# Two-layer hybrid backbone: the second layer's gate of the conditioning summed on VectorE, the first layer's on TensorE with 256 columns a group

## The chip, the cores and the metric

One core of a Trainium2 chip runs the whole forward pass as one program. The metric is the device time of one execution in microseconds (us), the median of the executions shown. Engine names are those of the profile: PE is TensorE's matmul, PEld its weight load, DVE is VectorE, ACT is ScalarE, POOL is GpSimd, SP is SyncE, which in this kernel issues nearly all DMAs, in one order.

## The reference, cut to what matters

`x` holds 1024 latent tokens and `ctx` 256 context tokens, both 1024 wide. Each of the two layers takes a shift, a scale and a gate from a conditioning vector. Context tokens have a conditioning vector of their own, and the second layer's context output is not needed.

```python
cond_l = silu(c)[:, None, :]          # latent tokens
cond_c = silu(c_ctx)[None, None, :]   # context tokens
for layer in range(2):
    shift_l, scale_l, gate_l = split(cond_l @ w_ada[layer] + b_ada[layer], 3)
    shift_c, scale_c, gate_c = split(cond_c @ w_ada[layer] + b_ada[layer], 3)
    hl = rms_norm(x, norm_g[layer]) * (1 + scale_l) + shift_l
    hc = rms_norm(xc, norm_g[layer]) * (1 + scale_c) + shift_c
    yl, yc = even_layer(hl, hc, ...) if layer == 0 else odd_layer(hl, hc, ...)
    x = x + gate_l * yl
    if layer == 0:
        xc = xc + gate_c * yc
return rms_norm(x, final_g)
```

`w_ada[layer]` is 1024 x 3072. So of the second layer's gate only the latent row counts, of the first layer's both rows.

## The kernel before

`run` (line 188) goes through the stages in order: `layer0_in`, `layer0_out`, `layer1_in`, `layer1_attention`, `layer1_out`. All products of activations and weights are made from a high and a low part (`mm3`, line 98: three matmuls, lines 100 to 102), with 512 columns for latent tokens (operand `h`) and 256 for context tokens (`h0c`).

The conditioning is computed inside `layer0_in`. The two conditioning vectors stand as two of 32 stationary columns in `cs` (line 253), one 128-row block `k` of eight after another. The first layer's shift and scale come from `ada_chunk` (line 262, matmuls of 256 columns at line 269). What is left are sixteen steps, made by `ada_steps` (line 411): eight for the second layer's shift and scale (bank 0, weights `w_ada1`) and then eight for the gates (bank 1, weights `w_adag`, in which each row holds 1024 columns of the first layer's gate and 1024 of the second's). Each step takes a block `wa` of 128 x 2048 (1 MB, loaded by `ada_load`, line 257, into one of three buffers) and makes four matmuls of 32 x 512 columns, one for each group of 32 columns of the array (`ada_step`, line 280, matmul at line 282), added up over the eight steps in one PSUM bank. Behind the eighth step `ada_end` (line 285) adds the bias `bt` (line 288). For bank 0 it transposes the sum (line 295) into the layer's scale and shift; for bank 1 it stores rows 0 and 1 of each group to `gate_d` in DRAM with four DMAs (line 291), which both layers later read back with `gate_tile` (line 305).

The steps are spread over the projections of the first layer: loop `j` over five weight blocks (K and four of Q, line 463), in each a loop over the token groups of 512, 512 and 256 columns, 24 matmuls to a group, with a step behind chunks 3 and 7 where the table `ADA` says so. A finished group goes to `rotated` (line 375): ACT copies it from PSUM to `qk` (line 380, three buffers), DVE shuffles it (383), POOL and DVE multiply by cosine and sine (384, 385), DVE adds (386), and a DMA stores it to `q_d` (388). The weight blocks are loaded as `raw` (line 146 or 130), cast on ACT to the high part (line 88, `w_hi`) and split on POOL (line 96, `w_lo`). Behind the steps come the weight block and the products of the next part, `sg` (lines 499 to 504), with Gelu on ACT.

In this stage no order is written out by hand: a scheduler that plans with a timeline of its own sets the order of instructions on every engine, from what is ready and from the order of the program. Every engine and SP then work in that order, so that an instruction that waits holds up all behind it on its engine. From the first layer's attention on (line 624) the order is the program's own.

Of the kernel before, what the change touches and what calls it, by code (L numbers as in the profile page):

```python
# [7 lines left out]
F32 = mybir.dt.float32  # L8
# [3 lines left out]
ALU = mybir.AluOpType  # L12
# [4 lines left out]
P = 128  # L17
D = 1024
KC = D // P
# [5 lines left out]
GROUPS = [(0, 512), (512, 512), (1024, 256)]  # L25
# [5 lines left out]
XB = 8  # L31
# [22 lines left out]
class Kernel:  # L54
# [227 lines left out]
            self.nc.tensor.matmul(ps[32 * g:32 * g + 32, 0:512], lhsT=self.cs[:, k, :],  # L282
                                  rhs=wa[:, g * 512:(g + 1) * 512], start=k == 0, stop=k == KC - 1)

    def ada_end(self, bank, ps):
        nc = self.nc
        at = self.t(self.wap, [P, 512], F32, "at", bufs=1)
        nc.vector.tensor_tensor(at, ps[:, 0:512], self.bt[:, bank], op=ALU.add)
        if bank == 1:
            for g in range(4):  # L290
                nc.sync.dma_start(self.gate_d[g], at[32 * g:32 * g + 2, :])
            return
        tp = ps
        for j in range(4):
            nc.tensor.transpose(tp[:, j * P:(j + 1) * P], at[:, j * P:(j + 1) * P], self.ident)
        ad = self.t(self.wap, [P, 4, 4, 2], F32, "ad", bufs=1)
        nc.vector.tensor_copy(ad, tp.rearrange("p (j g q) -> p j g q", j=4, g=4)[:, :, :, 0:2])
        for r in range(2):
            v = lambda a: a.rearrange("p (g j) -> p g j", g=2)
            w = lambda s: ad[:, :, s:s + 2, r].rearrange("p j g -> p g j")  # L300
            nc.vector.scalar_tensor_tensor(v(self.aT[1][:, r]), w(2), 1.0, v(self.ng[:, 1]),
                                           op0=ALU.add, op1=ALU.mult)
            nc.vector.tensor_copy(v(self.sT[1][:, r]), w(0))
# [8 lines left out]
    def layer0_in(self):  # L312
        nc, i = self.nc, self.i
# [5 lines left out]
        wp = self.pool(es_h, "w0")  # L319
# [16 lines left out]
        xp = self.pool(es_p, "xp", bufs=4, side="right")  # L336
        load_ = self.load
# [60 lines left out]
        def weights(j):  # L398
            return self.wblock(wp, i["w0"][8 + j], eng=("A", "G"), load=load_)

        ada = [(b, k) for b in range(2) for k in range(KC)]
        fetched = []

        def fetch(n):
            while len(fetched) < n and len(fetched) < len(ada):
                b, k = ada[len(fetched)]
                fetched.append(self.ada_load(i["w_ada1" if b == 0 else "w_adag"][k]))
# [3 lines left out]
        def ada_steps(n):  # L411
            for _ in range(n):
                if self.ada_done == len(ada):
                    return
                b, k = ada[self.ada_done]
                if k == 0:
                    self.ada_ps = self.psum("b", 2)
                fetch(self.ada_done + 2)
                self.ada_step(k, self.ada_ps, fetched[self.ada_done])
                self.ada_done += 1  # L420
                if k == KC - 1:
                    self.ada_end(b, self.ada_ps)


        xs = [xload(*GROUPS[0])]
        wa = [self.ada_load(i["w_ada0"][0])]
# [6 lines left out]
        ps = [self.bank() for _ in parts]  # L433
# [17 lines left out]
        load_(ca, i["ca"])  # L451
        load_(sa, i["sa"])
        for g in range(4):
            load_(self.bt[32 * g:32 * g + 2], i["bada"][g])
        fetch(2)
        norm(xs[2])
        for c in range(KC):
            modulated(xs[2], GROUPS[2], c)
            if c in ADA[0]:
                ada_steps(1)  # L460
        for b, (j, g, lag) in zip(ps, parts):
            rotated(j, b, GROUPS[g])
        for j in range(5):
            w = ws[j]
            for g, group in enumerate(GROUPS):
                if j < 2 and g < 2:
                    continue
                b = self.bank()
                for c in range(KC):
                    chunk(b, w, c, group)  # L470
                    if c in ADA[1 if j < 2 else 2 + g]:
                        ada_steps(1)
                rotated(j, b, group)
            if 0 < j < 4:
                ws.append(weights(j + 1))
        ada_steps(16)
        es_p.close()
        es_a.close()
        self.vt = self.pool(self.es_at, "v0", side="right").tile([P, NT, P], F32, name="vt")
# [16 lines left out]
        for hf in range(2):  # L496
            nc.sync.dma_start(bsb[64 * hf:64 * hf + 64], i["bs"][hf].partition_broadcast(64))

        w = self.wblock(wp, i["w0"][0])
        for j in range(4):  # L500
            wn = self.wblock(wp, i["w0"][j + 1]) if j < 3 else None
            for g0, gn in GROUPS:
                ps = self.project(w, hx, g0, gn)
                nc.scalar.activation(sg[:, j, g0:g0 + gn], ps, AF.Gelu)
            w = wn
            for k in WV[j]:
                raw = self.raw(i["wv"][k], [P, 640])
                self.hi("A", vwh[:, k], raw)
                self.lo("V", vwl[:, k], raw, vwh[:, k])
# [14 lines left out]
        for t in range(NT):  # L524
            ps = self.wide()
# [32 lines left out]
        bank = lambda: self.psum("b", 2)  # L558
# [1020 lines left out]
```

## Time and profile before

| | |
|---|---|
| median of three executions | 1503.92 us (1503.28 to 1504.01) |
| the profiled execution's own time | 1504.3 us |
| its span, first to last instruction | 1502.5 us |
| mean granted TensorE clock | 0.994 |
| PE busy | 1439.6 us, 96% |
| DVE busy | 879.5 us, 59% |
| ACT busy | 735.9 us, 49% |
| POOL busy | 397.4 us, 26% |

The span leaves 1.8 us of the execution outside the first and last instruction. Busy times are averages over stages; the conditioning steps all lie between 66 and 144 us of the span. In the timeline rows a matmul in fp32 shows as two records, so that a step of four matmuls reads x8 (x6 where records are missing), and the time that a step holds TensorE is read from the start of one matmul to the start of the next, since matmuls overlap in the rows.

### The profile page before, as it was taken

To read this page: it belongs to the slowest core of one execution; us is meant where nothing else is said; L and a number is where in the kernel's file an instruction comes from. 1 tells how busy PE (TensorE), PEld (TensorE's weight loads), DVE (VectorE), ACT (ScalarE), POOL (GpSimd) and SP (SyncE) were. 2 spreads that over 40 slices of the span, in tenths; PEclk is the share of its full clock that TensorE was granted. 3 is DMA by queue.
4 is the path that set the end of the run, shared out by engine and by line. 5 is a ranking of instruction groups with operands and counts; after the bars stand their busy time and mean duration, and the time that the engine had idled before them with its cause. 6 is when DMAs were issued, how large, how long until landed. Compare 5 with 4: busy or idle time off the path is not lost.

```text
span 1502.5 us, 23133 instructions
## 1 busy us (share of the span) xinstructions
PE 1439.6 (96%) x8849; PEld 1132.6 (75%) x8849; DVE 879.5 (59%) x1690; ACT 735.9 (49%) x1563; POOL 397.4 (26%) x351
## 2 busy tenths in 40 slices
PE   5999999999999799999998999999999999999998
PEld 3766899777666478879887777777777777776786
DVE  5582124356667877543745766676667666766454
ACT  4422310145567635443435766666666666676321
POOL 4243233223556533232470110011001100124100
PEclk9999999999999999999999999999999999999999
DMA  8557401222214646321231000000000000212241
GB/s 329 230 219 272 136 29 29 85 81 85 72 39 155 188 123 191 130 76 57 71 127 39 24 24 15 25 24 24 15 25 24 24 15 22 71 46 81 96 144 71
DMA packets 83783, 132.64 MB, mean 88 GB/s; under 512 B 7552, under 2 KB 59976, under 8 KB 80600
## 3 DMA queue, kind: packets, MB, share of 16 engines
q1 hardware_dynamic: 83528, 130.91, 25.9%
q8 instruction: 69, 1.13, 0.3%
q14 instruction: 42, 0.34, 0.1%
q10 hardware_dynamic: 144, 0.26, 0.0%
HBM read 99.59 MB, written 31.56 MB: 87 GB/s over the span
## 4 chain that ended last, share of the span: by engine, by line
PE 75%; DVE 9%; ACT 5%; issue 4%; DMA 4%; POOL 2%; SPq 0%; POOLq 0%; DVEq 0%; ACTq 0%
PE acc L1270 9%; PE tm L1252 7%; PE s L100 7%; PE s L101 7%; PE s L102 7%; PE b L100 5%; PE b L101 4%; PE b L102 4%; PE s L1215 3%; PE s L1216 3%; PE s L1217 3%; PE tm L100 2%; PE acc L774 2%; DVE peak L1227 2%; ACT prob L1242 2%
## 5 line engine op out<-in xcount | busy, mean ns | idle before, releaser
L1259 ACT COPY pt<-tm 128x512 f32<-128x512 f32 x192 | 112.4, 585 | 165.7 <-PE tm L1252 165.7
L1252 PE MATMUL tm<-ident,prob 128*128 128x128 f32 x1280 | 178.3, 273 | 7.8 <-ACT pt L1259 2.1
L1252 PEld LDWEIGHTS tm<-ident,prob 128*128 128x128 f32 x1280 | 150.8, 140 | 42.0 <-PE tm L1252 9.5
L1242 ACT ACTIVATE prob<-s,peak 128x1024 f32<-128x1024 f32 x128 | 143.3, 1120 | 38.0 <-DVE peak L1231 29.6
L1227 DVE TENSOR_REDUCE peak<-s 128x1 f32<-128x1024 f32 x128 | 155.0, 1211 | 1.8 <-PE s L1217 1.7
L1270 PE MATMUL acc<-pt,v 128*64 128x256 f32 x1280 | 152.0, 384 | 0.0
L96 POOL TENSOR_TENSOR ql<-pe,qh 32x512 fp32r<-32x512 f32 x32 | 40.7, 1271 | 413.2 <-ACT qh L88 386.2
L1261 DVE COPY pt<-tm 128x512 f32<-128x512 f32 x128 | 87.8, 686 | 79.4 <-PE tm L1252 77.4
L96 POOL TENSOR_TENSOR w_lo<-raw,w_hi 128x512 fp32r<-128x512 f32 (+1 forms) x60 | 74.9, 1261 | 199.0 <-DVE w_hi L90 98.5
L1270 PEld LDWEIGHTS acc<-pt,v 128*64 128x64 f32 x1280 | 86.3, 136 | 49.7 <-issue 9.6
L1215 PE MATMUL s<-kh,qh 96*128 96x512 f32 x256 | 109.2, 426 | 2.5 <-DVE raw L186 1.5
L1216 PE MATMUL s<-kl,qh 96*128 96x512 f32 x256 | 100.9, 394 | 0.0
L1217 PE MATMUL s<-kh,ql 96*128 96x512 f32 x256 | 100.8, 394 | 0.0
L1168 DVE TENSOR_TENSOR ql<-tm,qh 64x256 fp32r<-64x256 f32 x62 | 26.1, 421 | 83.7 <-ACT qh L1166 83.3
L100 PE MATMUL b<-h,yh 128*128 128x512 f32 x160 | 63.8, 399 | 3.7 <-ACT yh L88 2.7
L100 PE MATMUL s<-h,w_hi 128*128 128x512 f32 x160 | 63.9, 412 | 2.2 <-ACT qk L380 2.2
L101 PE MATMUL s<-h,w_hi 128*128 128x512 f32 x160 | 63.7, 398 | 0.3 <-DVE rs_v L125 0.3
L101 PE MATMUL b<-h,yh 128*128 128x512 f32 x160 | 63.3, 395 | 0.0
L102 PE MATMUL s<-h,w_lo 128*128 128x512 f32 x160 | 63.0, 395 | 0.0
L102 PE MATMUL b<-h,yl 128*128 128x512 f32 x160 | 62.5, 391 | 0.0
L1242 ACT ACTIVATE prob<-sx,peak 128x256 f32<-128x256 f32 x128 | 61.0, 477 | 0.6
L1217 PEld LDWEIGHTS s<-kh,ql 96*128 96x128 f32 x256 | 48.0, 188 | 11.2
(469 smaller groups left out, 3733.7 us busy)
## 6 DMA issues: line engine op xcount, KB each, us to landing
wa<-in_w_ada_dram SPq DMA_DIRECT2D x16, 1024.0 KB, 9.1
x<-in_xs_dram SPq DMA_DIRECT2D x20, 512.0 KB, 5.6
raw<-in_w_dram SPq DMA_DIRECT2D x17, 512.0 KB, 3.6
wa<-in_w_adag_dram SPq DMA_DIRECT2D x8, 1024.0 KB, 5.9
raw<-in_w_out_dram SPq DMA_DIRECT2D x10, 512.0 KB, 3.9
yf<-y_d SPq DMA_DIRECT2D x10, 512.0 KB, 5.6
x_d<-x SPq DMA_DIRECT2D x8, 512.0 KB, 4.5
raw<-in_w1g_dram SPq DMA_DIRECT2D x8, 512.0 KB, 3.4
```

The lines of the kernel that those rows point to most:

```text
L96: e.tensor_tensor(lo, src, hi.bitcast(F32), op=ALU.subtract)
L100: mm(out, lhsT=ah, rhs=bh, start=start, stop=False)
L101: mm(out, lhsT=ah, rhs=bl, start=False, stop=False)
L102: mm(out, lhsT=al, rhs=bh, start=False, stop=stop)
L1215: mm(o, lhsT=qh[0:96, q], rhs=kh[0:96, k0:k1], start=True, stop=False)
L1216: mm(o, lhsT=qh[0:96, q], rhs=kl[0:96, k0:k1], start=False, stop=False)
L1217: mm(o, lhsT=ql[0:96, q], rhs=kh[0:96, k0:k1], start=False, stop=True)
L1227: nc.vector.reduce_max(m[:, 0, a:a + 1], banks[n, a], axis=AX.X)
L1242: nc.scalar.activation(probs[n][j][:, TL:T] if c else probs[n][j][:, 0:TL], src, AF.Exp, bias=peaks[n][:, 2, j:j + 1], scale=scale, accum_ ...
L1252: nc.tensor.transpose(tp[:, o * P:(o + 1) * P], probs[n][j][:, k * P:(k + 1) * P], self.ident)
L1259: nc.scalar.copy(dst, src)
L1270: mm(accs[m][64 * e:64 * e + 64, 0:QG], lhsT=self.v4[hp // 2][:, kt, vc:vc + 64], rhs=pts[2 * m + e][:, kt], start=kt == 0, stop=kt == NT - 1)
```

## The change

The eight gate steps compute the two halves of a `wa` block in two ways. The first layer's 1024 columns go to TensorE as before, as four matmuls of 256 columns a step (`ada_gate_step`). The second layer's 1024 columns go to DVE: each step multiplies the 128 x 1024 half by the block's conditioning column (128 x 1) and adds it to a running total `ada_total`, which takes a buffer of the tag `x`. After the eighth step, `ada_gates` sums the total over its 128 partitions with four matmuls of 256 columns whose stationary operand is the constant `ones`, into the other half of the same bank, adds the bias, and stores eight pieces of 256 columns to `gate_d` in place of four of 512. The bias `bt` is loaded in twelve pieces in place of four. `ada_gates` stands behind the weight block and the first 512-column group of the next part's first product (`front`), which are moved ahead of the closing of the pools.

```diff
-    def ada_end(self, bank, ps):
+    def ada_gate_step(self, k, ps, total, wa):
+
+        nc = self.nc
+        for g in range(4):
+            nc.tensor.matmul(ps[32 * g:32 * g + 32, 0:256], lhsT=self.cs[:, k, :], rhs=wa[:, g * 256:(g + 1) * 256],
+                             start=k == 0, stop=k == KC - 1)
+        if k == 0:
+            nc.vector.tensor_scalar_mul(total, wa[:, D:2 * D], self.cs[:, k, 0:1])
+        else:
+            nc.vector.scalar_tensor_tensor(total, wa[:, D:2 * D], self.cs[:, k, 0:1], total, op0=ALU.mult, op1=ALU.add)
+
+    def ada_gates(self, ps, total):
+        nc = self.nc
+        for g in range(4):
+            nc.tensor.matmul(ps[32 * g:32 * g + 32, 256:512], lhsT=self.ones, rhs=total[:, g * 256:(g + 1) * 256],
+                             start=True, stop=True)
+        at = self.t(self.wap, [P, 512], F32, "at", bufs=1)
+        nc.vector.tensor_tensor(at, ps[:, 0:512], self.bt[:, 1], op=ALU.add)
+        for g in range(4):
+            c = slice(g % 2 * 256, g % 2 * 256 + 256)
+            nc.sync.dma_start(self.gate_d[g // 2][:, c], at[32 * g:32 * g + 2, 0:256])
+            nc.sync.dma_start(self.gate_d[2 + g // 2][:, c], at[32 * g:32 * g + 2, 256:512])
+
+    def ada_end(self, ps):
         nc = self.nc
         at = self.t(self.wap, [P, 512], F32, "at", bufs=1)
-        nc.vector.tensor_tensor(at, ps[:, 0:512], self.bt[:, bank], op=ALU.add)
-        if bank == 1:
-            for g in range(4):
-                nc.sync.dma_start(self.gate_d[g], at[32 * g:32 * g + 2, :])
-            return
+        nc.vector.tensor_tensor(at, ps[:, 0:512], self.bt[:, 0], op=ALU.add)
...
-                self.ada_step(k, self.ada_ps, fetched[self.ada_done])
+                wa = fetched[self.ada_done]
                 self.ada_done += 1
+                if b == 1:
+                    if k == 0:
+                        self.ada_total = self.t(xp, [P, D], F32, "x", bufs=XB)
+                    self.ada_gate_step(k, self.ada_ps, self.ada_total, wa)
+                    continue
+                self.ada_step(k, self.ada_ps, wa)
                 if k == KC - 1:
-                    self.ada_end(b, self.ada_ps)
+                    self.ada_end(self.ada_ps)
...
         for g in range(4):
-            load_(self.bt[32 * g:32 * g + 2], i["bada"][g])
+            load_(self.bt[32 * g:32 * g + 2, 0], i["bada"][g, :, 0])
+            c = slice(g % 2 * 256, g % 2 * 256 + 256)
+            load_(self.bt[32 * g:32 * g + 2, 1, 0:256], i["bada"][g // 2, :, 1, c])
+            load_(self.bt[32 * g:32 * g + 2, 1, 256:512], i["bada"][2 + g // 2, :, 1, c])
...
         ada_steps(16)
+        w = self.wblock(wp, i["w0"][0])
+        front = [self.project(w, hx, *GROUPS[0])]
+        self.ada_gates(self.ada_ps, self.ada_total)
         es_p.close()
         es_a.close()
...
-        w = self.wblock(wp, i["w0"][0])
         for j in range(4):
             wn = self.wblock(wp, i["w0"][j + 1]) if j < 3 else None
             for g0, gn in GROUPS:
-                ps = self.project(w, hx, g0, gn)
+                ps = front.pop(0) if front else self.project(w, hx, g0, gn)
                 nc.scalar.activation(sg[:, j, g0:g0 + gn], ps, AF.Gelu)
```

The scheduler's order changes with it between 66 and 146 us; from there on it is the same but for a few casts on ACT. Two places follow. Line numbers grow by 19 inside `layer0_in` of the changed kernel (383 becomes 402, 385 becomes 404, 386 becomes 405, 288 becomes 311, 388 becomes 407), and numbers behind names only tell one buffer from the next.

DVE's order before, where the fourth and fifth rotated groups of Q (`qk_984` and `qk_1073`) are followed by the bias of bank 0 (`at`):

```order
L383 STREAM_SHUFFLE hf_986<-qk_984 128x512
L385 TENSOR_TENSOR hf_986<-hf_986,x_689 128x512
L386 TENSOR_TENSOR qk_984<-qk_984,hf_986 128x512
L383 STREAM_SHUFFLE hf_1075<-qk_1073 128x512
L385 TENSOR_TENSOR hf_1075<-hf_1075,x_689 128x512
L386 TENSOR_TENSOR qk_1073<-qk_1073,hf_1075 128x512
L288 TENSOR_TENSOR at_1100<-b_916,bt 128x512
L383 STREAM_SHUFFLE hf_1133<-qk_1131 128x512
```

Here nothing but a rotation's own operands stands between its shuffle and its sum. The same place in the changed kernel:

```order
L402 STREAM_SHUFFLE hf_994<-qk_992 128x512
L404 TENSOR_TENSOR hf_994<-hf_994,x_689 128x512
L405 TENSOR_TENSOR qk_992<-qk_992,hf_994 128x512
L402 STREAM_SHUFFLE hf_1083<-qk_1081 128x512
L292 TENSOR_SCALAR x_1135<-wa_1102,cs 128x1024
L404 TENSOR_TENSOR hf_1083<-hf_1083,x_689 128x512
L405 TENSOR_TENSOR qk_1081<-qk_1081,hf_1083 128x512
L311 TENSOR_TENSOR at_1108<-b_924,bt 128x512
L294 SCALAR_TENSOR_TENSOR x_1135<-wa_1133,cs,x_1135 128x1024
L402 STREAM_SHUFFLE hf_1143<-qk_1141 128x512
L294 SCALAR_TENSOR_TENSOR x_1135<-wa_1162,cs,x_1135 128x1024
```

The first gate block's multiplication (L292, which needs the loaded `wa_1102`) now stands inside the rotation of `qk_1081`, and the next two additions stand around the shuffle behind it.

SP's order of DMAs before, from the last two blocks of bank 0 (`wa_1049`, `wa_1067`) to the weight block of loop `j` = 4 (`raw_1173`); `wa_1094`, `wa_1125`, `wa_1152` are the first three gate blocks:

```order
L130 DMA wa_1049<-in_w_ada_dram 128x2048
L130 DMA wa_1067<-in_w_ada_dram 128x2048
L130 DMA wa_1094<-in_w_adag_dram 128x2048
L388 DMA q_d<-qk_890 128x256
L388 DMA q_d<-qk_822 128x512
L388 DMA q_d<-qk_939 128x512
L388 DMA q_d<-qk_1023 128x256
L388 DMA q_d<-qk_984 128x512
L130 DMA wa_1125<-in_w_adag_dram 128x2048
L388 DMA q_d<-qk_1073 128x512
L130 DMA wa_1152<-in_w_adag_dram 128x2048
L130 DMA raw_1173<-in_w_dram 128x1024
```

Here the first gate block's load goes out ahead of the five stores. The same place in the changed kernel, where `wa_1102`, `wa_1133`, `wa_1162` are the first three gate blocks and `raw_1184` is the weight block of `j` = 4:

```order
L130 DMA wa_1057<-in_w_ada_dram 128x2048
L130 DMA wa_1075<-in_w_ada_dram 128x2048
L407 DMA q_d<-qk_898 128x256
L407 DMA q_d<-qk_830 128x512
L407 DMA q_d<-qk_947 128x512
L407 DMA q_d<-qk_1031 128x256
L407 DMA q_d<-qk_992 128x512
L130 DMA wa_1102<-in_w_adag_dram 128x2048
L130 DMA wa_1133<-in_w_adag_dram 128x2048
L407 DMA q_d<-qk_1081 128x512
L130 DMA wa_1162<-in_w_adag_dram 128x2048
L130 DMA raw_1184<-in_w_dram 128x1024
```

The first gate block's load has moved behind five stores of rotated groups, and the third gate block and the weight block stand behind the store of `qk_1081` as before.

## Rows read from the trace of the kernel before

**Rows 1.** The page: busy time of the engines, and the chain that ended last.
```profile
PE 1439.6 (96%) x8849; PEld 1132.6 (75%) x8849; DVE 879.5 (59%) x1690; ACT 735.9 (49%) x1563; POOL 397.4 (26%) x351
...
PE 75%; DVE 9%; ACT 5%; issue 4%; DMA 4%; POOL 2%; SPq 0%; POOLq 0%; DVEq 0%; ACTq 0%
```

**Rows 2.** Busy by stretch: length, each engine busy (count), clock, DMA share, GB/s.
```profile
100.00:120.00 20.00, 20.00 (x117) 12.79 (x116) 11.37 (x22) 3.08 (x6) 9.50 (x6) 1.00 0.72 270
120.00:140.00 20.00, 20.00 (x112) 13.42 (x111) 5.32 (x8) 4.98 (x9) 9.11 (x7) 1.00 0.80 315
```

**Rows 3.** Timeline of PE around a gate step: start, length, what [idle before <- releaser].
```profile
128.71 0.39 PE L102 MATMUL s<-h,w_lo 128*128 128x512 f32 x1
129.03 1.06 PE L282 MATMUL b<-wa,cs 128*32 128x512 f32 x8
...
130.36 0.39 PE L101 MATMUL s<-h,w_hi 128*128 128x512 f32 x1
```

**Rows 4.** Timeline of PE around four matmuls of 256 columns in `ada_chunk`.
```profile
51.94 0.40 PE L102 MATMUL s<-h,w_lo 128*128 128x512 f32 x1
52.26 0.63 PE L269 MATMUL b<-wa,cs 128*32 128x256 f32 x6
...
53.16 0.39 PE L101 MATMUL s<-h,w_hi 128*128 128x512 f32 x1
```

**Rows 5.** Timeline of PE, where it waited for a PSUM bank.
```profile
90.58 0.50 PE L100 MATMUL s<-h,w_hi 128*128 128x512 f32 x1 [2.23 <-ACT qk L380]
```

**Rows 6.** Timeline of ACT, the copy that released that bank.
```profile
89.95 0.85 ACT L380 COPY qk<-s 128x512 f32<-128x512 f32 x2
```

**Rows 7.** Groups of DVE instructions by shape: count | busy us, mean ns | idle.
```profile
L354 DVE TENSOR_SCALAR x<-x,rs_r 128x1024 f32<-128x1024 f32 x10 | 7.5, 750 | 0.1
L1497 DVE SCALAR_TENSOR_TENSOR o<-x,rs_r,fg 128x1024 f32<-128x1024 f32 x7 | 9.0, 1284 | 0.2
```

**Rows 8.** Timeline of DVE, rotations of Q.
```profile
100.86 1.78 DVE L385 TENSOR_TENSOR hf<-hf,x 128x512 f32<-128x512 f32 x1
...
107.42 0.69 DVE L385 TENSOR_TENSOR hf<-hf,x 128x512 f32<-128x512 f32 x1
109.28 0.69 DVE L386 TENSOR_TENSOR qk<-qk,hf 128x512 f32<-128x512 f32 x1 [1.17 <-POOL qk L384]
```

**Rows 9.** Timeline of SP, issues of DMAs.
```profile
94.06 12.96 SPq L388 DMA_DIRECT2D q_d<-qk  x5
107.12 0.38 SPq L130 DMA_DIRECT2D wa<-in_w_adag_dram  x1
...
110.42 0.38 SPq L130 DMA_DIRECT2D wa<-in_w_adag_dram  x1
110.89 0.40 SPq L130 DMA_DIRECT2D raw<-in_w_dram  x1
```

**Rows 10.** DMAs issued from 106 to 109 us: count, KB each, us to landing.
```profile
wa<-in_w_adag_dram SPq DMA_DIRECT2D x1, 1024.0 KB, 5.4
```

**Rows 11.** Timeline of ACT, the cast of the weight block of `j` = 4.
```profile
116.79 1.14 ACT L88 CAST w_hi<-raw 128x512 fp32r<-128x512 f32 x2 [3.57 <-DMA raw<-in_w_dram]
```

**Rows 12.** Timeline of PE, the first product of `j` = 4.
```profile
119.14 0.50 PE L100 MATMUL s<-h,w_hi 128*128 128x512 f32 x1
```

**Rows 13.** Timeline of SP, the bias loads and the first two steps' loads.
```profile
55.73 1.26 SPq L130 DMA_DIRECT2D bt<-in_bada_dram  x4
57.24 1.66 SPq L130 DMA_DIRECT2D wa<-in_w_ada_dram  x2
```

**Rows 14.** Timeline of PE, the first step of bank 0.
```profile
66.00 1.07 PE L282 MATMUL b<-wa,cs 128*32 128x512 f32 x8
```

**Rows 15.** Timeline of PE behind a pause at the start of attention.
```profile
294.00 0.78 PE L707 MATMUL s<-qs,kh 128*128 128x512 f32 x1 [2.49 <-POOL qs L96]
```

**Rows 16.** Busy by stretch behind that pause, columns as in rows 2.
```profile
294.00:296.00 2.00, 2.00 (x5) 1.62 (x6) 0.49 (x1) 0.00 (x0) 0.00 (x0) 0.51 0.49 158
296.00:298.00 2.00, 2.00 (x8) 1.57 (x7) 0.42 (x2) 1.36 (x4) 0.00 (x0) 0.64 0.72 234
```

## Prediction

> **What bounds the kernel now.** I read the page first: TensorE is busy for 96% of the span and carries 75% of the chain that ended last [rows 1]. The steps that change lie between 66 and 144 us, so the second view is the busy time by stretch: from 100 to 140 us PE has no idle time and the clock is at its upper level of 2.4 GHz, while DVE is busy for 11.37 and 5.32 of 20 us, and the DMA engines for 0.72 and 0.80 [rows 2]. So here TensorE time taken out is time won, DVE has room, and loads could become late. The third view is the timelines of PE, DVE, ACT and SP, which show in what order the waiting happens.
>
> **TensorE: what leaves.** A step of four matmuls of 512 columns: from the matmul ahead of it to the second one behind it 130.36 - 128.71 = 1.65 us [rows 3]; without the step the two ordinary gaps of 0.23 us (three matmuls of `mm3` take 0.69) would have stood there, so a step costs 1.65 - 0.46 = 1.19 us. The same four with 256 columns: 53.16 - 51.94 - 0.46 = 0.76 us [rows 4]. Eight gate steps save 8 x 0.43 = 3.4 us; the four new matmuls over `ada_total` have this second shape and cost 0.76. Net, TensorE has 2.7 us less to do.
>
> **TensorE: idle time that is there now.** PE waits 2.23 us at 90.58 for a bank that ACT's copy releases [rows 5, 6]. ACT makes that copy behind two weight casts now, and ahead of them in the changed order. I take 1.2 us of the 2.23 as won (bounds 0 and 2.2), if nothing behind it waits.
>
> **DVE: what comes.** One multiplication of 128 x 1024 (0.75 us) and seven multiply-adds (1.28 us each): 9.7 us [rows 7]. DVE is idle for some 23 us between 100 and 140 [rows 2], so the work itself costs nothing. What it waits for is another matter. The added instructions wait for the DMA of a `wa` block, and DVE works in order. In the changed order the first one stands inside a rotation, ahead of the multiplication by the sine and the sum (L404, L405). Behind that sum waits SP's store of it, and behind that store stand the load of the third gate block and that of the weight block of `j` = 4.
>
> **The chain that this makes, step by step.** In the kernel before, a run of five stores ends with a load issued at 107.12 [rows 9]; it lands 5.4 us later [rows 10]. In the changed order the first gate block's load is the one behind these five stores. DVE's work up to the fifth is the same set of instructions in another order, so I take 107.1 again, with bounds of 105.9 (the 1.17 us for which DVE waited for POOL here [rows 8] gone) and 108.2 (one more rotation held up like the 1.78 us against 0.69 [rows 8]).
>
> - The block lands at 112.5. Multiplication 0.75 [rows 7], sine 0.69, sum 0.69 [rows 8]: the sum is done at 114.65. Before, it was done at 109.28 + 0.69 = 109.97. That is 4.7 us later.
> - SP then issues store, third gate block and weight block. The third gate block goes from 110.42 to 115.1 and lands at 120.5, the weight block from 110.89 to 115.6 [rows 9].
> - The weight block was first used by ACT 5.9 us behind its issue, at 116.79 [rows 9, 11]: now 121.5. Half of the cast of two (1.14) is 0.57, so PE can start `j` = 4 at 122.0.
> - PE started it at 119.14 [rows 12]. It would start at 122.0, 2.9 us later. What PE saved ahead of this point (three gate steps, and the idle time at 90) it spends waiting: for bank 0's bias, which stands behind the same sum on DVE, for the third gate block, and for this weight block.
>
> Behind that point five shorter steps save 5 x 0.43 = 2.15 us and the four new matmuls take 0.76, so 1.4 us come back.
>
> **What else moves.** Eight more loads of the bias on SP, at 0.31 us each [rows 13], come ahead of the first step's load: 2.5 us or more later. The first step started 8.8 us behind its load's issue [rows 13, 14], and in the changed order ten products of 0.23 us stand ahead of it: I take 0, bounds 0 and 1. Four more stores of the gate, 1.3 us of SP: their reader comes a stage later, 0. The moved `front` is work that stood next in PE's order anyway, 0. The later gate blocks are loaded some 6 us or more ahead of their use, 0.
>
> **Sum.** Later by 2.9, back 1.4: +1.5 us on the profiled execution's own 1504.3 (span 1502.5), which stands 0.4 above the median of 1503.9. Against the median: 1505.4. A measurement of this kernel can tell about 0.2%, 3.0 us, from no change, so this counts as the same. With the bounds of the chain's start and 1 us either way for the landing, +0 to +4.
>
> **The rivals.**
>
> *The loads come in time* (chance 0.20). If the first gate block goes out by 102 us, for which its buffer must be free and the five stores done earlier, nothing waits, and the gain is all of it: 2.7 + 1.2 = 3.9 us, 1500.0. Against it: the run of stores holds SP for 12.96 us up to 107 [rows 9]. For it: the loads could land faster than 5.4 us when the rings are empty.
>
> *The pauses cost the clock* (0.25), slower. Behind a pause of 2.49 us PE's clock read 0.51 and then 0.64 in stretches of 2 us [rows 15, 16], partly the lower level of 1.2 GHz; that lost 0.98 + 0.72 = 1.7 us. Behind the pause of 2.23 us [rows 5] it did not fall. The chain above makes three pauses of about 2, 2 and 1 us within 10 us, at `at`, the third gate block and the weight block. If one of them brings the clock down, +1.5 becomes +3.2: 1507.1, and with the chain's start at its late bound 1508. It decides the sign from the point where PE spends 3 us at the lower level, which loses half of that, 1.5, and takes +1.5 to +3.0. The Trainium skill's page "TensorE: Matmul & The Clock Gate" (Part 1) has the clock throttled by default and only activity release it; the two pauses seen here, one with a fall and one without, agree with that and leave open which kind the three would be.
>
> *DVE and POOL get in each other's way* (0.05), slower by a little. The sine product took 1.78 us in one place and 0.69 in another [rows 8]. An addition of 1.28 us [rows 7] that meets the split of the weight block on POOL could hold it up by as much: +2.8, 1506.7. The Trainium skill's page "SBUF — State Buffer" ("SBUF: two separate sides") has the two engines share a pair of ports that one instruction holds to its end, and counts a DVE instruction with two inputs in SBUF among the holders; by that rule the seven additions each can stop POOL, where by the rows POOL has idle time around most of them.
>
> *256 columns save less than the rows show* (0.03): with 0.2 us a step in place of 0.43, the way back is 0.2 and not 1.4, +2.7, 1506.6.
>
> **How the numbers follow.** The forecast has 0.47. The rest is as above. Faster by over 0.2% (below 1500.9): 0.15 of the first rival and 0.02 of the forecast, 0.17. Slower by over 0.2% (above 1506.9): 0.18 of the clock rival, 0.06 of the forecast and 0.06 of the other two, 0.30. Same: 0.53. The range that holds 8 in 10 reaches from 1500.8, where it leaves out half of the first rival, to 1509.0, with the clock rival in its late bound.
>
> **What would show it.** In the profile after: the first gate block's load at about 107 us and landing near 112.5, DVE's L292 waiting for a DMA, its sum L405 at about 114; the store and the weight block's load near 115; PE idle between 112 and 122 us by 4 to 6 us, released by `at`, `wa` and `w_hi`; the first product of `j` = 4 near 122; gate steps of about 0.76 us. It would be wrong if PE shows no idle time there, if the weight block's load goes out near 111 as before, or if the clock falls below 1.00 between 110 and 130 us.

## The result, and the profile after

| | before | changed |
|---|---|---|
| median | 1503.84 us (1503.28 to 1504.12, 6 executions) | 1511.58 us (1510.67 to 1514.44, 6 executions) |
| ratio | | 1.0054, 95% interval 1.0041 to 1.0067 |
| profiled execution | 1504.3 us, span 1502.5 | 1514.44 us, span 1512.7 |
| mean granted clock of the spans | 0.994 (profiled) | 0.990 (profiled), 0.991 to 0.992 (the other five) |

The change makes the kernel slower: by 0.54% by the ratio, by 7.7 us between the medians. The forecast was 1505.4 with a range up to 1509.0, and no change as the likeliest outcome. It was wrong, and the range did not hold the time. The profiled execution of the changed kernel is the slowest of its six, 2.9 us above their median. A second profile of the same kernel (experiment e10) shows which part of it is its own.

The page has the engines' totals, which answer to [rows 1]: PE is busy 6.6 us longer than before although it has less to do, in part because a matmul at half the clock counts for longer (the first product of `j` = 4, below, 0.80 us for 0.50 in [rows 12]).

```profile
PE 1446.2 (96%) x8857; PEld 1137.9 (75%) x8857; DVE 891.5 (59%) x1698; ACT 736.0 (49%) x1563; POOL 399.5 (26%) x351
```

The view by stretch answers to [rows 2], where PE had no idle time and the clock stood at 1.00 (columns as there, PE's busy time first, and a clock of 0.50 is the lower level):

```profile
114.00:116.00 2.00, 1.75 (x15) 0.82 (x13) 1.55 (x3) 0.59 (x1) 0.00 (x0) 1.00 0.86 365
116.00:118.00 2.00, 0.84 (x7) 0.85 (x8) 2.00 (x3) 0.00 (x0) 0.00 (x0) 1.00 0.33 121
118.00:120.00 2.00, 2.00 (x21) 1.45 (x20) 0.96 (x3) 0.00 (x0) 0.96 (x1) 1.00 0.66 199
120.00:122.00 2.00, 0.83 (x8) 0.63 (x6) 0.00 (x0) 0.00 (x0) 0.33 (x1) 1.00 1.00 377
122.00:124.00 2.00, 0.64 (x8) 0.16 (x8) 0.93 (x1) 0.00 (x0) 0.00 (x0) 1.00 1.03 418
124.00:126.00 2.00, 0.98 (x2) 0.83 (x3) 2.00 (x5) 1.65 (x4) 0.95 (x1) 0.53 1.05 442
126.00:128.00 2.00, 2.00 (x7) 1.67 (x6) 2.00 (x3) 0.80 (x2) 2.00 (x2) 0.50 1.00 397
128.00:130.00 2.00, 2.00 (x6) 1.52 (x6) 2.00 (x3) 0.00 (x0) 2.00 (x3) 0.50 0.94 309
130.00:132.00 2.00, 2.00 (x9) 1.60 (x8) 1.28 (x2) 0.00 (x0) 1.60 (x1) 0.76 1.06 416
```

PE stands idle for 5.0 us between 114 and 126, and then the clock is at its lower level of 1.2 GHz for most of 8 us. By the stretches alone that would be (0.47 + 0.50 + 0.50 + 0.24) x 2 = 3.4 us, but in the first of them PE worked for only 0.98 us, and a low clock costs nothing while PE stands. The timeline tells the price: the first sixteen matmuls of `j` = 4, from 125.02 to 131.29, take 6.27 us, and the same sixteen in the kernel before, from 119.14 [rows 12] to 122.72, take 3.58. The fall costs 2.7 us.

```profile
131.29 0.39 PE L100 MATMUL s<-h,w_hi 128*128 128x512 f32 x1
```

(The kernel before:)

```profile
122.72 0.39 PE L100 MATMUL s<-h,w_hi 128*128 128x512 f32 x1
```

The waits of PE from 66 to 150 us say what it stood for (us in total, times, longest):

```profile
PE b L289 <- DMA wa<-in_w_adag_dram: 2.2, 1, 2.2
PE b L314 <- DVE at L311: 1.4, 1, 1.4
PE s L100 <- ACT w_hi L88: 1.4, 1, 1.4
PE s L100 <- ACT qk L399: 0.8, 1, 0.8
PE b L282 <- DMA wa<-in_w_ada_dram: 0.5, 1, 0.5
```

The first three are the third gate block, the bias and the weight block of `j` = 4, as the prediction had named them. DVE's timeline shows the first gate block's multiplication (L292) inside the rotation, between its shuffle and its sum (L405):

```profile
108.38 0.73 DVE L402 STREAM_SHUFFLE hf<-qk 128x512 f32<-128x512 f32 x1
114.36 0.76 DVE L292 TENSOR_SCALAR x<-wa,cs 128x1024 f32<-128x1024 f32 x1 [5.25 <-DMA wa<-in_w_adag_dram]
115.03 0.69 DVE L404 TENSOR_TENSOR hf<-hf,x 128x512 f32<-128x512 f32 x1
115.81 0.69 DVE L405 TENSOR_TENSOR qk<-qk,hf 128x512 f32<-128x512 f32 x1
```

SP's timeline answers to [rows 9] and [rows 13]. The twelve bias loads hold SP for 8.79 us where four held it for 1.26, the first step's load goes out at 64.67 in place of 57.24, and the first gate block at 108.89:

```profile
55.84 8.79 SPq L130 DMA_DIRECT2D bt<-in_bada_dram  x12
64.67 0.83 SPq L130 DMA_DIRECT2D wa<-in_w_ada_dram  x2
...
98.05 10.75 SPq L407 DMA_DIRECT2D q_d<-qk  x5
108.89 0.88 SPq L130 DMA_DIRECT2D wa<-in_w_adag_dram  x2
116.53 0.33 SPq L407 DMA_DIRECT2D q_d<-qk  x1
117.38 0.33 SPq L130 DMA_DIRECT2D wa<-in_w_adag_dram  x1
117.81 0.40 SPq L130 DMA_DIRECT2D raw<-in_w_dram  x1
```

ACT's cast and PE's start of `j` = 4 answer to [rows 11] and [rows 12]: 124.35 for 116.79, and 125.02 for 119.14, 5.9 us later.

```profile
124.35 1.14 ACT L88 CAST w_hi<-raw 128x512 fp32r<-128x512 f32 x2 [9.29 <-DMA raw<-in_w_dram]
```

```profile
125.02 0.80 PE L100 MATMUL s<-h,w_hi 128*128 128x512 f32 x1 [1.36 <-ACT w_hi L88]
```

A later mark that both kernels have, the first store of `u_d` on SP, lies at 213.67 before and at 220.88 after, 7.2 us later. That is the later start of `j` = 4 (5.9), the fall of the clock (2.7), and the 1.4 us that come back behind it. Behind this mark the work is the same in both kernels.

### The profile page after: what moved, and what is told of

Read it like the earlier page. It is cut to its first block, busy times and chain, and to the rows that moved or that the text cites. A ratio compares the mean times of both kernels' runs of the same rounds, so it can differ in the third digit from the quotient of the medians.

```text
span 1512.7 us, 23175 instructions
## 1 busy us (share of the span) xinstructions
PE 1446.2 (96%) x8857; PEld 1137.9 (75%) x8857; DVE 891.5 (59%) x1698; ACT 736.0 (49%) x1563; POOL 399.5 (26%) x351
## 4 chain that ended last, share of the span: by engine, by line
PE 72%; DVE 9%; ACT 5%; issue 3%; DMA 2%; POOL 0%; SPq 0%; POOLq 0%; DVEq 0%; ACTq 0%
PE acc L1300 9%; PE tm L1282 7%; PE s L100 7%; PE s L101 7%; PE s L102 7%; PE b L100 5%; PE b L101 4%; PE b L102 4%; PE s L1245 3%; PE s L1246 3%; PE s L1247 3%; PE acc L804 2%; PE tm L100 2%; DVE peak L1257 2%; ACT prob L1272 1%
```

## The experiments

Two theories stood at the start. By A the twelve bias loads are what costs: they delay SP, and the scheduler therefore places the first gate block's load behind the five stores. By B it is DVE's additions, which wait for a DMA inside the rotations, wherever the bias comes from. The kernel before ran beside every experiment; its medians there were 1504.8 to 1505.4 us, so ratios are compared. Differences in us are worked out from the ratios where nothing else is said.

| run | ratio to before (95%) | first gate block issued | weight block `j` = 4 issued | PE waits, 110 to 126 us |
|---|---|---|---|---|
| changed | 1.0054 (1.0041 to 1.0067) | 108.89 | 117.81 | 1.4 + 2.2 + 1.4 |
| e10 changed, again | 1.0042 (1.0028 to 1.0055) | 108.37 | 117.29 | 1.4 + 2.1 + 1.3 |
| e1 four bias loads | 0.9983 (0.9974 to 0.9992) | 88.62 | 111.75 | none |
| e2 before, twelve bias loads | 1.0010 (1.0001 to 1.0019) | 108.83 | 112.96 | 2.3 |
| e3 all additions behind the sums | 1.0006 (0.9996 to 1.0015) | 108.42 | 112.54 | 0.4 + 1.3 |
| e4 no additions | 1.0005 (0.9996 to 1.0015) | 107.18 | 111.28 | 0.8 + 1.3 |
| e5 twelve bias loads, later | 0.9988 (0.9977 to 1.0000) | 87.58 | 110.77 | 2.5 |
| e6 four loads, additions behind the sums | 0.9988 (0.9979 to 0.9996) | 89.04 | 111.48 | none |
| e7 as e6, four `qk` buffers | 1.0010 (1.0000 to 1.0020) | 106.83 | 110.21 | 2.2 + 1.7 |
| e8 before, product moved | 0.9999 (0.9989 to 1.0009) | 89.04 | 111.50 | none |
| e9 first addition behind its sum | 1.0005 (0.9996 to 1.0014) | 107.65 | 111.78 | 0.6 + 1.3 |
| e11 four loads later, weight block ahead | 0.9984 (0.9975 to 0.9993) | 87.76 | 77.44 | 0.5 + 0.2 |

**e1, four bias loads.**

```diff
-            load_(self.bt[32 * g:32 * g + 2, 0], i["bada"][g, :, 0])
...
+            load_(self.bt[32 * g:32 * g + 2], i["bada"][g])
...
-    banks = [[b[1, j] for j in range(4)], [b[0, 4], b[0, 5], b[1, 4], b[1, 5]]]
+    gates = [[b[l, 4 + g // 2, g % 2 * 256:g % 2 * 256 + 256] for l in range(2)] for g in range(4)]
+    banks = [[b[1, j] for j in range(4)], [np.concatenate(pair) for pair in gates]]
```

> The changed kernel, with the bias laid out on the host in the new order of its columns, so that four loads bring it as before instead of twelve; the additions on DVE, the 256-column steps and the moved first product stay. Theory A (the twelve bias loads are what costs): with four of them SP issues the first gate block's load ahead of the run of five stores again, near 88 us in place of 108.9; DVE never waits for a DMA inside a rotation, the weight block of j = 4 goes out near 111 in place of 117.8, PE's three pauses between 115 and 125 us are gone and the clock stays at 1.00 there. The gain of the prediction's first rival is then all there is: 2.7 + 1.2 to 1.4 us, 1500 us (1499 to 1501.5). Theory B (the additions on DVE inside the rotations are what costs, wherever the bias comes from): the waits move but stay, 1507 to 1512 us.

1502.17 us, ratio 0.9983: 2.6 us faster than before (1.2 to 3.9), and 9 to 11 us faster than the changed kernel (its ratios in e10 and in the first comparison). SP's order up to the first additions is that of the kernel before:

```profile
88.62 0.33 SPq L130 DMA_DIRECT2D wa<-in_w_adag_dram  x1
94.30 13.64 SPq L407 DMA_DIRECT2D q_d<-qk  x5
...
111.75 0.42 SPq L130 DMA_DIRECT2D raw<-in_w_dram  x1
```

PE's waits from 66 us on are two: that for a tile at 66, and the one at 90 us, which is there in full, as in [rows 5]:

```profile
PE s L100 <- ACT qk L399: 2.2, 1, 2.2
PE tm L379 <- DVE x L373: 1.0, 1, 1.0
```

So without the twelve loads the change does what its arithmetic says, the net 2.7 us of TensorE. Theory A's number, 1500, was 2.2 us too low, of which 1.2 to 1.4 is the wait at 90 us: it is 2.2 us long with four loads, and 0.8 in the changed kernel, e2, e3 and e9, where the twelve loads stand ahead of the steps.

**e2, the kernel before with twelve bias loads.**

```diff
-            load_(self.bt[32 * g:32 * g + 2], i["bada"][g])
+            load_(self.bt[32 * g:32 * g + 2, 0], i["bada"][g, :, 0])
+            load_(self.bt[32 * g:32 * g + 2, 1, 0:256], i["bada"][g, :, 1, 0:256])
+            load_(self.bt[32 * g:32 * g + 2, 1, 256:512], i["bada"][g, :, 1, 256:512])
```

> The kernel before, with one edit: its bias is loaded in twelve pieces in place of four, and nothing else of the change is there. Theory A: SP is held up in these loads as in the changed kernel (8.8 us in place of 1.3 us), the first gate block's load falls behind the five stores, to about 108.5 us, and PE waits for gate blocks near 113 and 118 us by 2 to 4 us; there are no additions on DVE that the stores could wait for, so the weight block of j = 4 goes out near 112 to 113. Expected 1506.5 us (1505 to 1509; the upper end if the pauses bring the clock down). Theory B: small loads of 2 to 4 KB cost nothing that matters, 1503.9 us (1503 to 1504.8).

1506.12 us, ratio 1.0010: 1.5 us slower (0.2 to 2.9). The direction and place are A's (bias loads 7.55 us, first gate block at 108.83, weight block at 112.96), the size is at its lower end. The twelve loads alone are a small loss, and cannot be the 7.7 us by themselves; and e1 shows that neither can the additions. What costs is the two together. (The profile of e2 is of its slowest execution, 3.1 us above its median; the clock fell there behind the pause of 2.3 us.)

**e3 and e4, the additions out of the rotations, and out altogether.**

```diff
-            nc.vector.tensor_scalar_mul(total, wa[:, D:2 * D], self.cs[:, k, 0:1])
+            ins = nc.vector.tensor_scalar_mul(total, wa[:, D:2 * D], self.cs[:, k, 0:1])
...
+        self.tc.add_manual_dep(ins.ins, self.summed.ins.name,
+                               mybir.DependencyInfo(mybir.DependencyClass.NoSync, mybir.DependencyReason.DATA),
+                               reason="sum first")
...
-                nc.vector.tensor_tensor(d, d, sh, op=ALU.add)
+                self.summed = nc.vector.tensor_tensor(d, d, sh, op=ALU.add)
```

> The changed kernel with its twelve bias loads, with each addition on DVE ordered behind the last sum of a rotation that stands ahead of it in the program, so that no store waits for a gate block's load through DVE. Theory A: the first gate block still goes out near 109 us and lands near 114, but the sum is done near 110 and the weight block of j = 4 goes out near 112 in place of 117.8; the pause for it (1.4 us) goes, that for the third gate block (2.2 us) shrinks to below 1, and if the clock then stays up its 3.4 us come back too: 1504 us (1501.5 to 1507). Theory B: the same direction and more, all that was lost comes back, 1500 us (1499 to 1501.5), since the bias loads cost nothing.

```diff
-            nc.vector.tensor_scalar_mul(total, wa[:, D:2 * D], self.cs[:, k, 0:1])
-        else:
-            nc.vector.scalar_tensor_tensor(total, wa[:, D:2 * D], self.cs[:, k, 0:1], total, op0=ALU.mult, op1=ALU.add)
+            nc.vector.memset(total, 0.0)
```

> The changed kernel with its twelve bias loads and without the eight additions on DVE: the total is set to zero once, so the second layer's gate is left out of the computation; its four matmuls, the bias and the stores are still made. Nothing on DVE waits for a gate block. Theory A: the gate blocks 1 and 2 go out near 109 as in the changed kernel, TensorE waits for the first of them by up to 2 us at about 114, the third and the weight block of j = 4 are near 112: 1503.5 us (1501 to 1506). Theory B: 1500 us (1499 to 1501.5). If it comes out as the changed kernel, 1510 us or more, both are wrong and the cost lies with the 256-column steps or the moved product.

1504.80 and 1504.58 us, ratios 1.0006 and 1.0005: with the additions behind the sums the kernel is as fast as with no additions at all, within the intervals (e4 leaves the second layer's gate out of the result, and the scheduler's order moves in it elsewhere too, with the first step at 67.50 for 69.13 in e3). By the ratios 5 to 7 us of the loss lie in where the additions stand and not in their work, with the first gate block nearly as late as in the changed kernel (108.42 and 107.18). Both times lie in theory A's ranges; theory B's 1500 did not come.

**e9, one instruction moved by two places.** As e3, but only the first multiplication (L292) is ordered behind the sum. The orders on SP, PE, ACT and POOL are the changed kernel's.

```diff
-            nc.vector.tensor_scalar_mul(total, wa[:, D:2 * D], self.cs[:, k, 0:1])
+            ins = nc.vector.tensor_scalar_mul(total, wa[:, D:2 * D], self.cs[:, k, 0:1])
+            self.tc.add_manual_dep(ins.ins, self.summed.ins.name,
...
```

> The changed kernel, twelve bias loads and all, with one instruction of one engine moved by two places: DVE's first multiplication of a gate block stands behind the sum of the fifth rotated group, not ahead of its product by the sine; the orders on SP, PE, ACT and POOL are the changed kernel's. If the chain of the prediction is what turns the late gate block into lost time (the store, the third gate block's load and the weight block's load all wait for that sum), the sum is done near 110 in place of 116.5 us, the weight block goes out near 112.5 in place of 117.8, the pauses shrink to those of the kernel with all additions behind the sums (1.3 and 0.4 us, and up to 1 for the bias) and the clock stays up: ratio 1.0005 to 1.002. If the other seven additions matter as much, or the lateness of the gate blocks alone, the ratio stays at 1.004 to 1.006.

1505.52 us, ratio 1.0005, beside 1.0042 for e10 in the same comparison. DVE's sum (L408 here) comes before the wait, and SP goes on. (The row of L292 names PE as what ended its wait; the gate block went out at 107.65 and, with 5.5 us to land as in the changed kernel, would be there at about 113.2, an estimate.)

```profile
109.78 0.69 DVE L408 TENSOR_TENSOR qk<-qk,hf 128x512 f32<-128x512 f32 x1 [1.18 <-POOL qk L406]
113.21 0.76 DVE L292 TENSOR_SCALAR x<-wa,cs 128x1024 f32<-128x1024 f32 x1 [2.74 <-PE s L102]
```

```profile
110.50 0.33 SPq L410 DMA_DIRECT2D q_d<-qk  x1
111.34 0.33 SPq L130 DMA_DIRECT2D wa<-in_w_adag_dram  x1
111.78 0.40 SPq L130 DMA_DIRECT2D raw<-in_w_dram  x1
```

PE's pauses are 0.6 and 1.3 us, and its clock stays at 1.00 behind them:

```profile
118.00:120.00 2.00, 0.94 (x11) 0.25 (x9) 1.08 (x1) 0.00 (x0) 1.27 (x1) 1.00 1.05 426
120.00:122.00 2.00, 1.15 (x6) 0.98 (x6) 2.00 (x4) 1.41 (x3) 1.13 (x1) 1.00 1.05 434
122.00:124.00 2.00, 2.00 (x11) 1.54 (x10) 2.00 (x4) 1.15 (x2) 2.00 (x3) 1.00 0.98 414
```

This is the chain DVE, store, load, cast, taken apart at one link: of the 6.3 us that e10 loses by its ratio, 5.6 hang on it (5.4 between the two medians), the fall of the clock included.

**e10, the changed kernel again.** No edit.

> The changed kernel itself, beside the others and on their chip. Ratio 1.0054 as before (1.004 to 1.007). The question is the clock: if its fall behind the three pauses near 125 us belongs to this order of work and not to one execution, this profile shows a granted clock near 0.5 for some 6 us there again, and the fall near 815 us of the first profile, which nothing of the change explains, is absent.

1510.89 us, ratio 1.0042. The same three pauses, and the clock falls again, for a shorter time: the same sixteen matmuls of `j` = 4, from 124.40 to 129.49, take 5.09 us for 3.58, so the fall costs 1.5.

```profile
124.00:126.00 2.00, 1.60 (x4) 1.31 (x5) 2.00 (x3) 2.00 (x5) 1.58 (x2) 0.60 1.03 434
126.00:128.00 2.00, 2.00 (x8) 1.67 (x7) 2.00 (x4) 0.17 (x1) 2.00 (x2) 0.55 1.01 422
128.00:130.00 2.00, 2.00 (x11) 1.65 (x10) 2.00 (x3) 0.00 (x0) 1.90 (x2) 1.00 1.02 378
```

From 800 to 840 us the first profile's clock read 0.91 and this one's 1.00. So the fall near 125 us came in both profiles of this order of work, at a price of 1.5 and 2.7 us, and that near 815 us belonged to one execution, the slowest. The sum at the first store of `u_d` holds here too: 5.3 us for the start of `j` = 4, 1.5 for the clock, 1.4 back, and the store at 219.05, 5.4 us later than before.

**e5, the place of the twelve loads.** They move from ahead of the first step's load to behind the weight block of `j` = 3.

```diff
-        for g in range(4):
-            load_(self.bt[32 * g:32 * g + 2, 0], i["bada"][g, :, 0])
...
+            if j == 2:
+                for g in range(4):
+                    load_(self.bt[32 * g:32 * g + 2, 0], i["bada"][g, :, 0])
```

> The changed kernel with all its twelve bias loads, but these moved in the program from ahead of the first step's load to behind the load of the weight block of j = 3 (near 76 us), where TensorE needs nothing from SP for some time; the bias is first used near 110 us. If it is the place of the twelve loads that costs (SP stands in them for 7 to 9 us while the first step's blocks wait behind them), the first gate block goes out ahead of the five stores again and the time is that of the kernel with four loads: 1502.2 us, a ratio to the kernel before of 0.998 to 0.999. If it is their number, wherever they stand, SP stands in them near 80 to 90 us instead, the first gate block falls behind the stores as in the changed kernel, and the ratio is 1.003 to 1.006.

1502.19 us, ratio 0.9988, as with four loads. SP stands in them for 6.67 us, nearly as long, where nothing needs it, and the gate block goes out at 87.58:

```profile
75.77 6.67 SPq L130 DMA_DIRECT2D bt<-in_bada_dram  x12
85.08 0.36 SPq L407 DMA_DIRECT2D q_d<-qk  x1
85.86 1.19 SPq L130 DMA_DIRECT2D wa<-in_w_ada_dram  x2
87.58 0.33 SPq L130 DMA_DIRECT2D wa<-in_w_adag_dram  x1
```

It is not the number of loads that costs but what waits behind them. (Its profile is of its slowest execution, with a pause of 2.5 us and a fall of the clock to 0.59 behind it.)

**e6, e7, e11, versions meant to be faster.** e6 joins the edits of e1 and e3. e7 is e6 with one buffer more for the rotated groups (`bufs=4` for `bufs=3` in the pool `rp`). e11 is e1 with its four bias loads where e5 has them, and the load of the weight block of `j` = 4 issued with them.

> Both mends at once: four bias loads, and each addition on DVE ordered behind the last sum of a rotation ahead of it. If, with four loads, the additions cost nothing any more (each block has landed when DVE comes to its addition), this is the same as with four loads alone: ratio 0.998 (0.997 to 0.999). If some addition still holds up a store in that kernel, this is 1 to 2 us faster: 0.9975 or below.

> The last kernel with four buffers for the rotated groups in place of three. The pause of 2.2 us at 90 us that is left with four bias loads (TensorE waits for a bank until ACT copies it, and that copy waits for a buffer and stands behind two casts) should go or shrink to below 1 us: 1.2 to 2.2 us less than the last kernel, ratio 0.9965 to 0.998. Against it: the run of stores on SP changes its order, with the first gate block behind six stores; if that makes loads late again it is slower than the last kernel, up to 1.002.

> A version that may beat both: four bias loads with the new layout, placed behind the load of the weight block of j = 3, and the load of the weight block of j = 4 (only the load, its casts stay) issued with them, so that neither the first steps' blocks wait behind the bias nor the weight block behind the store. The first step starts near 65 us in place of 66.2, TensorE is 1 to 1.3 us ahead from there, and with the weight block early nothing takes that back: ratio 0.9972 to 0.998 (four bias loads alone gave 0.9983). If the gate blocks or the casts behind the early weight block become late in its place, it is no better than four bias loads alone, 0.998 to 1.000.

e6: 1502.74 us, 0.9988. With four loads the place of the additions costs nothing that the ratios tell: in e1 DVE comes to the first block at 103.58 and does not wait, and its waits for later blocks (0.7 to 2.0 us) leave PE without one. e7: 1506.37 us, 1.0010, worse than e6 by 3.3 us. The wait at 90 us falls to 0.6, but the scheduler, with another buffer free, puts the first gate block behind six stores (106.83 us), and 2.2 + 1.7 us of pauses return, with the clock at 0.50 behind them. e11: 1502.59 us, 0.9984, no better than e1. e1, e11 and e6 beat both kernels, the kernel before by 0.17% (0.08 to 0.26), 0.16% (0.07 to 0.25) and 0.12% (0.04 to 0.21).

**e8, the moved product alone**, in the kernel before.

```diff
-        ada_steps(16)
+        ada_steps(15)
+        w = self.wblock(wp, i["w0"][0])
+        front = [self.project(w, hx, *GROUPS[0])]
+        ada_steps(1)
```

> The kernel before with one edit: the weight block and the first 512-column product of the next part are moved ahead of the last gate step and of the closing of the pools, as in the change; nothing else of it. By the prediction this moves work that stood next on TensorE anyway and costs and gains nothing: ratio 0.9993 to 1.0007. If the closing of the pools held up something, it gains up to 1 us.

1504.95 us, ratio 0.9999. It costs nothing.

## Why the prediction was wrong, step by step

**What was right.** The 2.7 us net of TensorE (e1: 2.6). The chain, link by link: the landing 5.5 us behind the issue (5.4 taken), multiplication, product and sum 2.1 us, then store, third gate block and weight block in that order. "PE idle between 112 and 122 us by 4 to 6 us, released by `at`, `wa` and `w_hi`": 5.0 us by these three, between 114 and 126. The moved product and DVE's own work at nothing (e8, e4).

**The step that failed first**: "Eight more loads of the bias on SP, at 0.31 us each ... I take 0, bounds 0 and 1." They were priced as issues. SP waits in them: from 55 to 66 us its waits were 1.3 us for the loads of two `x` tiles, 3.0 for that of `ca` and 1.0 for that of `sa`, half a megabyte each and issued just ahead of the bias. These waits stand before the fifth to the eighth bias load (57.23, 58.64, 61.93 and 63.2), so that each of these loads went out when the one eight places ahead of it in SP's order had landed. Before, SP waited for the same four transfers, but with the first two steps' blocks going out at 57.24 and 58.54, behind the waits for the two `x` tiles alone. The first step's load came 7.4 us later, where the text had "2.5 us or more". The slack of 8.8 us behind it [rows 13, 14] was real for that step (it waited only 0.5 us), but the work after it moved. DVE, busy for 1.9 of every 2 us from 90 to 98 us in both kernels, does its work there in another order, and comes to the fourth group's shuffle at 101.87 for 99.64 and ends the fifth group's sum at 108.5 for 106.7, 1.8 us later; e2, with nothing of the change but the twelve loads, has the shuffle at 101.81 and the sum at 108.4. The first gate block's issue, "107.1 again, with bounds of 105.9 ... and 108.2", became 108.9 (108.4 in e10), outside the bounds: "the same set of instructions in another order" took longer. And the reordering that the text took as given, the gate block behind five stores, was itself the twelve loads' doing: with four loads it is not there (e1), and with the twelve alone it is (e2). The order of the changed kernel was read, but not what in the change had caused it.

**The step that was mis-sized**: the start of `j` = 4, "122.0, 2.9 us later". It was 125.0, 5.9 later. Of the 3.0 us between, 1.8 is that issue, 0.4 SP's way from the store to the weight block's load (1.28 us for the 0.89 taken), 0.6 that block's landing (cast 6.5 us behind the issue, not 5.9), and 0.2 the start behind the cast and rounding. From 54 us to that start, by stretch:

```profile
54.00:119.14 65.14, 61.53 (x364) 43.08 (x362) 47.31 (x90) 22.00 (x40) 28.48 (x23) 1.00 0.74 279
```

```profile
54.00:125.02 71.02, 63.52 (x365) 43.33 (x364) 48.18 (x88) 21.54 (x40) 26.93 (x21) 0.99 0.65 249
```

(The first is the kernel before.) PE's idle time is 7.50 us for 3.61, 3.9 more, and it is busy 2.0 us longer although three steps of 0.43 less lie in it. So 3.3 us of TensorE time came that no term of the sum had. Two more broken steps of bank 0 explain about 2.0 (last section); what made the remaining 1.3 is not shown.

**The rival that came true with it**: "The pauses cost the clock", which had 0.25. The clock fell in both profiles of this kernel, at 1.5 and 2.7 us where 1.7 had been priced. Late start and fall together are 3.0 + 2.7 = 5.7 us above the forecast, 1511.1; the measured median is 1511.6. The rival alone, 1507.1 to 1508, would still have been too low: the start of `j` = 4 was the larger part.

**The idle time at 90 us**, 1.2 taken as won: it fell from 2.23 to 0.78, 1.45. The size was right, and so was the order on ACT from which it was read (the copy at 89.36, ahead of the casts). What moved that order had not been asked: the wait does not shrink in e1, and does in e2, so the twelve loads did it. The loads-in-time rival (0.20, 1500.0) is what e1 is, at 1502.2.

**DVE and POOL.** One addition met the four pieces in which POOL made the low part of the weight block, and took 2.30 us for its 1.28:

```profile
128.15 2.30 DVE L294 SCALAR_TENSOR_TENSOR x<-wa,cs,x 128x1024 f32<-128x1024 f32 x1
```

```profile
125.05 6.56 POOL L96 TENSOR_TENSOR w_lo<-raw,w_hi 128x512 fp32r<-128x512 f32 x4 [4.72 <-ACT w_hi L88]
```

POOL's four pieces took 6.56 us here (5.47 in e10) and 4.99 in e2, which has no additions. The Trainium skill's page "SBUF — State Buffer" ("SBUF: two separate sides") has the two share a pair of ports that one instruction holds to its end while the other waits, and counts a DVE instruction with two inputs in SBUF among the holders, against a GpSimd instruction that reads SBUF. The rows agree: 2.30 lies between the addition alone, 1.28, and the addition behind a whole piece, 1.28 + 1.28. It cost nothing that the runs can tell: e4, without the additions, is no faster than e3.

## What to carry to other kernels

Price a small load by what its queue waits for when it gets there, not by its issue: ask which earlier transfers must have landed, and which load the row of small ones delays. Where an instruction that waits for a DMA joins an in-order engine, look which store stands behind it and which loads stand behind that store; e9 won 5.6 us by moving one instruction two places. Where a scheduler's order moved, find the part of the change that moved it (order the kernel with that part alone) before pricing the order as given.

## What the runs showed of the hardware

A step of four matmuls that is broken in two costs nearly twice. In the changed kernel, one matmul of a step stands alone at 95.69 (two records), and a whole step at 110.38:

```profile
95.38 0.39 PE L102 MATMUL s<-h,w_lo 128*128 128x512 f32 x1
95.69 1.05 PE L282 MATMUL b<-wa,cs 128*32 128x512 f32 x2
96.67 0.39 PE L100 MATMUL s<-h0c,w_hi 128*128 128x256 f32 x1
...
110.06 0.39 PE L102 MATMUL s<-h,w_lo 128*128 128x512 f32 x1
110.38 1.07 PE L282 MATMUL b<-wa,cs 128*32 128x512 f32 x8
111.37 0.50 PE L100 MATMUL s<-h,w_hi 128*128 128x512 f32 x1
```

From the matmul ahead to the one behind it is 1.29 us for one and 1.31 for four. Less the ordinary gap of 0.23 us each piece costs about 1.1. So four matmuls on four column groups cost together what a lone one costs. With the twelve loads the scheduler breaks three steps of bank 0 (at 73, 85 and 96 us), where the kernel before has one broken: two more pieces of about 1 us. e2, which has nothing of the change but the twelve loads, breaks the same three, and e1 one.

The length of a pause did not decide by itself whether the clock fell. Behind the pause of 2.2 us at 90 us in the kernel before [rows 5] it read 1.00 in every 2 us up to 96; behind 2.3 us in e2 and 2.5 in e5 it read 0.71 and 0.50, and 0.59 and 0.56; behind 1.4, 2.2 and 1.4 within 11 us it fell in both profiles of the changed kernel, and behind 0.6, 1.7 and 1.7 within 10 us in e7, to 0.50; behind 0.6 and 1.3 in e9 it did not. Most of these are one trace each, and nothing here shows how often a kernel's executions differ in it.
